# Nine instead of five column pairs of the up-projection by seven block products, their weight sums made earlier and parked in DRAM

## The chip, the cores and the metric

The kernel runs on one core of a Trainium2 chip. A core has a matmul engine (TensorE, PE in the profile), a vector engine (VectorE, DVE), a scalar engine (ScalarE, ACT), GpSimd (POOL), and a sync engine (SyncE, SP) whose queue issues most of the transfers between DRAM and the core's on-chip memory. Each engine works through its own queue; semaphores tie the queues together. [...]

The metric is the device time of one launch in microseconds: 726.13 us is the median of three runs before (726.13 to 726.62).

## What is computed

One block of a streaming encoder, for 512 frames of width 1024, all in float32:

```python
hn = rms_norm(x, norm1_g)
proj = hn @ w_in                  # q, k, v of branch A and of branch B, gates A and B
out_a = chunked_attention(qa, ka, va, ...)        # 8 heads x 64, softmax
out_b = stick_breaking_attention(qb, kb, vb)      # 8 heads x 64, strictly causal
mixed = sigmoid(gate_a) * (out_a @ w_branch_a) + sigmoid(gate_b) * (out_b @ w_branch_b)
x = x + mixed @ w_out
x = x + conv_glu(rms_norm(x, norm2_g), w_ffn_up, ffn_conv_w, ffn_conv_b, w_ffn_down)

def conv_glu(x, w_up, conv_w, conv_b, w_down):
    hid = x @ w_up                # 1024 -> 2 x 2816
    hid = causal_depthwise_conv(hid, conv_w) + conv_b      # width 3
    gate, up = hid[..., :D_FF], hid[..., D_FF:]
    return (silu(gate) * up) @ w_down
```

The change is in the line `hid = x @ w_up` and in the preparation of its weights.

## The kernel before

**Three matmuls for one.** Each float32 operand is split into a high half (a cast to the matmul's float32r format) and a low half (the rest), and each product is high by high, high by low, and low by high: three matmuls (`mm3`, L251). So each weight chunk of 128 x 2048 is loaded (`load`, L113, an SP transfer into one of two `raw` buffers) and then split: ScalarE copies it to `whi` and VectorE subtracts to get `wlo` (`split_gen`, L204). `run_chunk` (L242) runs the matmuls of one chunk and lets the split of the next chunk go on beside them; at the end of a split, `split_gen` issues the load of the chunk two ahead.

**Order of the chunks** (`_chunks`, L37): input projection and attention first, then `yB0`, `yB1` (the branch products), `wo0` to `wo3` (output projection), then `up0` to `up21`, and the 22 passes of the down-projection.

**Attention.** The loop at L726 goes through 64 steps, 32 for branch A and then 32 for branch B: eight heads by four blocks of 128 queries. A step has score matmuls, a chain on ScalarE and VectorE (softmax for A; two sigmoids, a reversed scan, a product and a mask on POOL for B, L622), transposes of the block on TensorE (L651), and the high and low halves of the transposed block (L664, L665). Steps start three ahead of their use. The chunks of the input projection are dealt out among the steps (`fill_gen`), so that TensorE has matmuls beside the chains. What belongs to a step is ranked 100 places ahead (`HP`).

**Up-projection.** Chunk `up{j}` holds 128 gate columns and the 128 up columns that go with them (a column pair). An ordinary pair (`up_body`, L935) is 2 x 8 x 3 = 48 matmuls with 512 frames as the moving operand. After it come the conv (`conv`, L849: one ScalarE pass, two VectorE passes each for gate and up), the SiLU, the product (L928), and for each two pairs the sums that the down-projection wants (`pair_sums`, L870). Seven of the eleven y sums are stored to DRAM by POOL (`ayd`, L933) and fetched back from j = 18 on (`fetch`, L948).

A pair in `SEVEN` (L63: 5, 8, 11, 14, 17) is done by seven block products in place of eight (`up_seven`, L986): the weights are taken as 2 x 2 blocks of 128 x 512 (two halves of the 1024 inputs by gate and up) and the frames as two halves of 256. Each product is 4 x 3 = 12 matmuls with 256 moving columns, so 84 in all, and five VectorE adds of 256 columns and four ScalarE copies put the results together. It needs three sums of weight blocks (S1, S2, S4) and one difference that takes the place of a block, and sums of the frames (`token_sums`, L960, made once during `up1` to `up3`). The weight sums are made by VectorE during the pair before (`block_sums`, L173, called at the end of the split of the pair before, L237), into the tile `sx`; `split_seven` (L188) then makes high and low halves of the four blocks (into `whi`, `wlo`) and of the three sums (into `wxh`, `wxl`). These are four VectorE sums of 512 columns, two more casts on ScalarE (1024 and 512 columns) and two more subtractions on VectorE than an ordinary pair has.

**Queues.** The order on each engine is laid down ahead of the run from the program's order, the ranks and the data dependences; at run time each engine follows its queue, and an instruction that waits holds those behind it. SP's queue has the weight loads, bias tiles, rows of x and results; POOL's the masks and the y sums.

Of the kernel before, what the change touches and what calls it, by code (L numbers as in the profile page):

```python
# [8 lines left out]
F32 = mybir.dt.float32  # L9
# [53 lines left out]
SEVEN = (5, 8, 11, 14, 17)  # L63
# [3 lines left out]
def block_kernel(ctx: ExitStack, tc: tile.TileContext, x, xt, params, g2, rbx, wts, wd0, wd1, out):  # L67
# [17 lines left out]
    pool_c = apool("pc")  # L85
    par = sm.tile([P, 280], F32, tag="par", name="par")
# [22 lines left out]
    raws, splits, late = {}, {}, {"halves": (), "casts": (), "products": ()}  # L109
# [3 lines left out]
    def load(i, parts=1):  # L113
# [14 lines left out]

        cuts = [0, *parts, 8] if isinstance(parts, tuple) else [8 * j // parts for j in range(parts + 1)]
# [43 lines left out]
    def block_sums(i):  # L173

        b = raws[i].rearrange("p (b c) -> p b c", c=512)
        sx = late["pool"].tile([P, 1536], F32, tag="sx", name=f"sx_{order[i]}")
        late["sx"] = sx
        s1, s2, s4 = (sx[:, 512 * j:512 * (j + 1)] for j in range(3))
        V.tensor_tensor(s1, b[:, 1], b[:, 3], op=ALU.add)
        yield  # L180
        V.tensor_tensor(s2, s1, b[:, 0], op=ALU.subtract)
        yield
        V.tensor_tensor(s4, b[:, 2], s2, op=ALU.subtract)
        yield
        V.tensor_tensor(b[:, 1], b[:, 0], b[:, 1], op=ALU.subtract)
        yield

    def split_seven(i, raw, hi, lo):  # L188

        key = order[i]  # L190
        wh, wl = (late["pool"].tile([P, 1600], F32R, tag=tag, name=f"{tag}_{key}")[:, 16:1552]
                  for tag in ("wxh", "wxl"))
        splits[key] = tuple(t.rearrange("p (k c) -> p k c", c=P) for t in (hi, lo, wh, wl))
        sx = late["sx"]
        for j, (h, l, src) in enumerate(((hi[:, 0:1024], lo[:, 0:1024], raw[:, 0:1024]),
                                         (wh[:, 0:1024], wl[:, 0:1024], sx[:, 0:1024]),
                                         (hi[:, 1024:2048], lo[:, 1024:2048], raw[:, 1024:2048]),
                                         (wh[:, 1024:1536], wl[:, 1024:1536], sx[:, 1024:1536]))):
            A.copy(h, src)
            V.tensor_tensor(l, src, h.bitcast(F32), op=ALU.subtract)  # L200
            if j < 3:
                yield

    def split_gen(i, pieces):  # L204
# [5 lines left out]
        raw = raws.pop(i)  # L210
        sh = 48 if key[:2] in ("qA", "kA", "vA", "vB") else 16 if key in ("up0", "up1") or is_seven(i) else 0
# [28 lines left out]
    pos = {k: i for i, k in enumerate(order)}  # L240
# [24 lines left out]
    ayd = dram.tile([7, P, 1536], F32, tag="ayd", name="ayd")  # L265

# [355 lines left out]
    def soft_b(h, t, ps):  # L622
# [8 lines left out]
        A.activation(b[:, :n], ps[:, :n], AF.Sigmoid, scale=rstd[:, t:t + 1])  # L631
# [74 lines left out]
    pend = []  # L706

# [18 lines left out]
    for s in range(len(steps)):  # L726
# [40 lines left out]
    for i in range(2):  # L767
        for _ in run_chunk(f"yB{i}", yB_body(i)):
            pass
# [56 lines left out]
    for c in range(3):  # L826
        for _ in run_chunk(f"wo{c}", wo_body(c)):
            pass
# [6 lines left out]
    for _ in sp:  # L835
        pass
    ap_ctx.close()
# [110 lines left out]
    def fetch(i):  # L948

        tag = {0: "sx", 1: "wxl"}.get(i, "ts" if i < 5 else "ax")  # L950
        n, bufs = {"sx": (1536, 1), "wxl": (1600, 1), "ts": (2048, 4), "ax": (2048, 8)}[tag]
# [299 lines left out]
```

## Time and profile before

| | |
|---|---|
| time, median of 3 runs | 726.13 us (726.13 to 726.62) |
| span of the profiled execution, first to last instruction | 724.9 us |
| TensorE busy / VectorE / ScalarE / POOL | 718.6 / 565.4 / 401.5 / 53.6 us |
| moved by DMA | 100.91 MB, mean 139 GB/s |
| TensorE's granted clock | 1.000 |

The time of the profiled execution as a whole is not among the records, only its span; the runs' median is 1.2 us above that span. Lines such as L254 are those of the listing above. A group's row gives the engine, the operation, output<-inputs by the names of their tiles, the shapes, the count, then the busy microseconds and the mean of one in nanoseconds, then the engine's idle time just before and what ended it. Rows of one tile give least, median and most nanoseconds instead. SPq is the queue on which SP issues transfers.

### The profile page before, as it was taken

What the parts mean: (1) busy time and instruction counts of PE and PEld (TensorE: products, weight loads), DVE (VectorE), ACT (ScalarE), POOL (GpSimd) and SP (SyncE); (2) the same over time, 40 slices, a digit from 0 to 9 for tenths busy, and PEclk for the clock granted to TensorE, in tenths of its full rate; (3) what the DMA queues carried; (4) which work ended last, traced back from release to release, by engine and by line L of the source; (5) the groups of instructions that cost most, each with busy time, mean ns of one, the idle gap of its engine ahead of it and who ended that gap; (6) DMA issues with size and microseconds to landing.
All of it is one profiled execution on the core that took longest, in us unless ns stands there. A gap on an engine that the chain in (4) does not pass through costs nothing.

```text
span 724.9 us, 10589 instructions
## 1 busy us (share of the span) xinstructions
PE 718.6 (99%) x4019; PEld 627.5 (87%) x4019; DVE 565.4 (78%) x1030; ACT 401.5 (55%) x727; POOL 53.6 (7%) x95
## 2 busy tenths in 40 slices
PE   8999999999999999999999999999999999999997
PEld 8999998888988888888889889889898988888886
DVE  6678867775988888566275799998979985997686
ACT  6675656657767676442254556655545653543541
POOL 2701200000101011000012000000000100000000
PEclk9999999999999999999999999999999999999999
DMA  8632232211313111314536613544335553564563
GB/s 308 250 131 78 83 117 74 74 59 58 118 63 113 59 59 59 136 68 144 195 149 239 203 62 156 186 135 160 118 145 186 181 184 117 173 243 174 177 222 116
DMA packets 24786, 100.91 MB, mean 139 GB/s; under 512 B 2592, under 2 KB 7328, under 8 KB 17184
## 3 DMA queue, kind: packets, MB, share of 16 engines
q1 hardware_dynamic: 21792, 87.00, 33.8%
q0 software_dynamic: 2656, 13.11, 5.0%
q8 instruction: 31, 0.51, 0.3%
q14 instruction: 19, 0.16, 0.1%
q10 hardware_dynamic: 288, 0.14, 0.1%
HBM read 88.44 MB, written 11.80 MB: 138 GB/s over the span
## 4 chain that ended last, share of the span: by engine, by line
PE 98%; DMA 1%; SPq 0%; DVE 0%; ACT 0%; DVEq 0%; issue 0%
PE P L1087 14%; PE p L998 7%; PE pg L254 4%; PE pg L253 4%; PE pg L255 4%; PE pu L254 4%; PE pu L255 4%; PE pu L253 4%; PE qkB L255 2%; PE gB L255 2%; PE qkB L253 2%; PE gA L253 2%; PE gA L254 2%; PE gB L253 2%; PE gA L255 2%; PE qkB L254 2%
## 5 line engine op out<-in xcount | busy, mean ns | idle before, releaser
L253 PE MATMUL pg<-hth,whi_up 128*128 128x512 f32 (+1 forms) x152 | 55.7, 367 | 0.0
L255 PE MATMUL pg<-hth,wlo_up 128*128 128x512 f32 (+1 forms) x152 | 55.7, 366 | 0.0
L254 PE MATMUL pg<-htl,whi_up 128*128 128x512 f32 (+1 forms) x152 | 55.7, 366 | 0.0
L254 PE MATMUL pu<-htl,whi_up 128*128 128x512 f32 (+1 forms) x152 | 55.6, 366 | 0.0
L253 PE MATMUL pu<-hth,whi_up 128*128 128x512 f32 (+1 forms) x152 | 55.6, 366 | 0.0
L255 PE MATMUL pu<-hth,wlo_up 128*128 128x512 f32 (+1 forms) x152 | 55.6, 365 | 0.0
L1087 PE MATMUL P<-whi_dn,ax 128*128 128x512 f32 x176 | 54.4, 389 | 0.0
L149 ACT CAST whi_dn<-raw_dn 128x1024 fp32r<-128x1024 f32 x33 | 34.3, 1051 | 25.5 <-PE P L1087 15.2
L145 DVE TENSOR_TENSOR wlo_dn<-raw_dn,whi_dn 128x1024 fp32r<-128x1024 f32 x33 | 40.0, 1224 | 9.2 <-ACT whi_dn L149 9.1
L228 DVE TENSOR_TENSOR wlo_up<-raw_up,whi_up 128x1024 fp32r<-128x1024 f32 (+1 forms) x40 | 41.2, 1062 | 7.0 <-ACT whi_up L226 7.0
L226 ACT CAST whi_up<-raw_up 128x1024 fp32r<-128x1024 f32 (+1 forms) x40 | 34.5, 917 | 14.7 <-PE pu L254 7.9
L1087 PE MATMUL P<-whi_dn,ay 128*128 128x512 f32 x132 | 40.8, 389 | 0.0
L1087 PEld LDWEIGHTS P<-whi_dn,ax 128*128 128x128 f32 x176 | 33.0, 188 | 6.8
L1087 PE MATMUL P<-wlo_dn,ax 128*128 128x512 f32 x88 | 34.2, 389 | 0.0
L254 PEld LDWEIGHTS pu<-htl,whi_up 128*128 128x128 f32 x152 | 28.6, 188 | 4.7
L253 PEld LDWEIGHTS pu<-hth,whi_up 128*128 128x128 f32 x152 | 28.5, 188 | 4.7
L255 PEld LDWEIGHTS pg<-hth,wlo_up 128*128 128x128 f32 x152 | 28.6, 188 | 4.7
L255 PEld LDWEIGHTS pu<-hth,wlo_up 128*128 128x128 f32 x152 | 28.5, 188 | 4.6
L253 PEld LDWEIGHTS pg<-hth,whi_up 128*128 128x128 f32 x152 | 28.6, 188 | 4.6
L254 PEld LDWEIGHTS pg<-htl,whi_up 128*128 128x128 f32 x152 | 28.6, 188 | 4.5
L633 DVE TENSOR_TENSOR_SCAN aB<-aB,reset 128x127 f32<-128x127 f32 (+3 forms) x32 | 26.0, 817 | 6.7 <-ACT aB L628 6.7
L1087 PEld LDWEIGHTS P<-whi_dn,ay 128*128 128x128 f32 x132 | 24.8, 188 | 5.1
(303 smaller groups left out, 2240.3 us busy)
## 6 DMA issues: line engine op xcount, KB each, us to landing
raw_up<-in_wts SPq DMA_DIRECT2D x22, 1024.0 KB, 4.8
raw_dn<-in_wd SPq DMA_DIRECT2D x11, 1024.0 KB, 4.8
raw_dn<-in_wd SPq DMA_DIRECT2D x11, 512.0 KB, 3.4
ayd<-ay POOLq DMA_DIRECT2D x7, 768.0 KB, 5.2
ay<-ayd POOLq DMA_DIRECT2D x7, 768.0 KB, 6.5
raw_gA<-in_wts SPq DMA_DIRECT2D x4, 1024.0 KB, 4.7
raw_qkB<-in_wts SPq DMA_DIRECT2D x4, 1024.0 KB, 4.8
raw_gB<-in_wts SPq DMA_DIRECT2D x4, 1024.0 KB, 4.7
```

What stands on the lines that cost most here:

```text
L145: chain("halves", V.tensor_tensor(o, x, y, op=op))
L149: chain("casts", A.copy(hi[:, sl], src))
L226: A.copy(hi[:, sl], raw[:, sl])
L228: E.tensor_tensor(lo[:, sl], raw[:, sl], hi[:, sl].bitcast(F32), op=ALU.subtract)
L253: PE.matmul(ps, sh, mh, start=first, stop=False)
L254: PE.matmul(ps, sh, ml, start=False, stop=False)
L255: PE.matmul(ps, sl, mh, start=False, stop=last)
L633: V.tensor_tensor_scan(ar, ar, reset[:, S - n:S - 1][:, ::-1], 1.0, op0=ALU.mult, op1=ALU.max)
L998: PE.matmul(ps, st, mv[:, k, :], start=first and k == 0 and n == 0, stop=last and k == 3 and n == 2, skip_group_check=True)
L1087: chain("products", PE.matmul(dst, st, mv, start=first and n == 0, stop=last and n == 2, skip_group_check=True))
```

## The change

1. `SEVEN` grows from (5, 8, 11, 14, 17) to (5, 7, 8, 10, 11, 12, 13, 15, 17): nine pairs are done by seven products, thirteen stay ordinary.
2. `block_sums` is gone. A new generator, `park_gen`, makes the sums of all nine pairs earlier, through one raw tile and one sum tile (`pkr`, `pks`). For a pair it loads the raw weights (1 MB), makes S1, the difference, S2 and S4 on VectorE, then three times a high half on ScalarE and a low half on VectorE, and stores the difference, the high halves and the low halves to a DRAM array `parked`.
3. One call of `park` makes one step of that generator (one load, one sum, or one cast with its subtraction), ranked 100 places behind. There is one call in each attention step from 8 to 49, two for each piece of `yB1` and of `wo0`, and one for each piece of `wo1` and `wo2`.
4. In the up-projection the raw load of a seven-product pair is three pieces (two blocks from the weights, the difference from `parked`), and `fetch_extra` loads the high and low halves of the sums (768 KB each) straight from `parked` into the tiles that TensorE reads. `split_seven` keeps only the halves of the four blocks.
5. The halves of pairs 7, 10 and 12 go into a second pair of tiles (`w2`), the others into `wxh` and `wxl`. For 5, 7, 8, 10 and 11 the fetch is issued at the end of the split of the pair before; for 12, 13, 15 and 17 (`LATE`) at the start of the pair's own split, which runs during the pair before. The first fetched y sum has a tile of its own (`wf`) in place of `sx`.

```diff
-SEVEN = (5, 8, 11, 14, 17)
+SEVEN = (5, 7, 8, 10, 11, 12, 13, 15, 17)
+EXTRA_AT = (7, 10, 12)
+LATE = (12, 13, 15, 17)
...
+        if is_seven(i):
+            n = SEVEN.index(i - pos["up0"])
+            SP.dma_start(raw[:, 0:512], wts[i, :, 0:512])
+            SP.dma_start(raw[:, 512:1024], parked[n, :, 0:512])
+            SP.dma_start(raw[:, 1024:2048], wts[i, :, 1024:2048])
+            yield
+            return
...
-    def block_sums(i):
-
-        b = raws[i].rearrange("p (b c) -> p b c", c=512)
-        sx = late["pool"].tile([P, 1536], F32, tag="sx", name=f"sx_{order[i]}")
...
+    def park_gen():
+
+        for n, j in enumerate(SEVEN):
+            i = pos[f"up{j}"]
+            raw = pool_pk.tile([P, 2048], F32, tag="pkr", name=f"pkr{j}")
+            sx = pool_pk.tile([P, 1536], F32, tag="pks", name=f"pks{j}")
+            behind(SP.dma_start(raw, wts[i]), (a_exps + b_sigs)[-1:])
+            yield
+            b = raw.rearrange("p (b c) -> p b c", c=512)
+            s1, s2, s4 = (sx[:, 512 * k:512 * (k + 1)] for k in range(3))
+            for o, x, y, op in ((s1, b[:, 1], b[:, 3], ALU.add), (b[:, 1], b[:, 0], b[:, 1], ALU.subtract),
+                                (s2, s1, b[:, 0], ALU.subtract), (s4, b[:, 2], s2, ALU.subtract)):
+                V.tensor_tensor(o, x, y, op=op)
+                yield
+            SP.dma_start(parked[n, :, 0:512], b[:, 1])
+            for k, (src, hi) in enumerate(((s1, b[:, 3]), (s2, b[:, 0]), (s4, b[:, 2]))):
+                A.copy(hi.bitcast(F32R), src)
+                V.tensor_tensor(src.bitcast(F32R), src, hi, op=ALU.subtract)
+                SP.dma_start(parked[n, :, 512 * (k + 1):512 * (k + 2)], hi)
+                yield
+            SP.dma_start(parked[n, :, 2048:3584], sx)
+
+    def fetch_extra(j):
+
+        n = SEVEN.index(j)
+        if j in EXTRA_AT:
+            wh, wl = (t[:, 16:1552] for t in late["w2"])
+        else:
+            wh, wl = (late["pool"].tile([P, 1600], F32R, tag=tag, name=f"{tag}_up{j}")[:, 16:1552]
+                      for tag in ("wxh", "wxl"))
+        SP.dma_start(wh.bitcast(F32), parked[n, :, 512:2048])
+        SP.dma_start(wl.bitcast(F32), parked[n, :, 2048:3584])
+        extras[j] = wh, wl
...
     def split_seven(i, raw, hi, lo):
...
+        wh, wl = extras.pop(i - pos["up0"])
+        splits[order[i]] = tuple(t.rearrange("p (k c) -> p k c", c=P) for t in (hi, lo, wh, wl))
+        for j in range(2):
+            sl = slice(1024 * j, 1024 * (j + 1))
+            A.copy(hi[:, sl], raw[:, sl])
+            V.tensor_tensor(lo[:, sl], raw[:, sl], hi[:, sl].bitcast(F32), op=ALU.subtract)
+            if j == 0:
                 yield
...
         raw = raws.pop(i)
+        if i - pos["up0"] in LATE:
+            fetch_extra(i - pos["up0"])
...
+        j = i + 1 - pos["up0"]
+        if j in SEVEN and j not in LATE:
+            fetch_extra(j)
         yield
-        if is_seven(i + 1):
-            yield from block_sums(i + 1)
...
+    def park():
+        with tc.high_priority(-LOW):
+            next(pk, None)
+
+    LOW = 100
...
+        if 8 <= s < 50:
+            park()
         br, h, t, e = pend.pop(0)
...
         for _ in run_chunk(f"yB{i}", yB_body(i)):
-            pass
+            if i == 1:
+                park()
+                park()
...
     for c in range(3):
         for _ in run_chunk(f"wo{c}", wo_body(c)):
-            pass
+            park()
+            if c == 0:
+                park()
...
+        late["w2"] = [fp.tile([P, 2048], F32R, tag="ax", name=f"w2{k}", bufs=8) for k in range(2)]
```

More of the change, by code (lines that the diff above doesn't have):

```diff
@@ L85, in block_kernel @@
     pool_c = apool("pc")
+    pool_pk = apool("ppk")
     par = sm.tile([P, 280], F32, tag="par", name="par")
@@ L107, in block_kernel @@
     order = [key for key, _, _ in CHUNKS]
-    raws, splits, late = {}, {}, {"halves": (), "casts": (), "products": ()}
+    pos = {k: i for i, k in enumerate(order)}
+    raws, splits, extras, late = {}, {}, {}, {"halves": (), "casts": (), "products": ()}
     FIRST_DN = order.index("dn0_0")
@@ L171, in is_seven @@
         return i < len(order) and order[i] in [f"up{j}" for j in SEVEN]
-    def block_sums(i):
-        b = raws[i].rearrange("p (b c) -> p b c", c=512)
-        sx = late["pool"].tile([P, 1536], F32, tag="sx", name=f"sx_{order[i]}")
[L177 to L186, printed above, removed]
@@ L188, in split_seven @@
-    def split_seven(i, raw, hi, lo):
[L190 to L201, printed above, removed]
+    def park_gen():
[18 more added lines that the diff above has]
+            SP.dma_start(parked[n, :, 2048:3584], sx)
@@ L265, in block_kernel @@
     ayd = dram.tile([7, P, 1536], F32, tag="ayd", name="ayd")
+    parked = dram.tile([len(SEVEN), P, 3584], F32, tag="parked", name="parked")
     reset = pool_c.tile([P, S], F32, tag="reset", name="reset")
@@ L836, in block_kernel @@
         pass
+    assert next(pk, 1) == 1
     ap_ctx.close()
```

8 lines of the change are left out of this document (4 added, 4 removed).

## The prediction

> **What bounds the kernel now.** I read the page first, then the waits of the matmul engine, then the chain of waits over the up-projection, and last the stages in which the added work falls. The page's first parts:
>
> ```profile
> span 724.9 us, 10589 instructions
> ...
> PE 718.6 (99%) x4019; PEld 627.5 (87%) x4019; DVE 565.4 (78%) x1030; ACT 401.5 (55%) x727; POOL 53.6 (7%) x95
> ```
>
> TensorE is busy for 99% of the span. A busy matmul engine could still be waiting between starts, so the second view is everything that it waited for, over the whole span:
>
> ```profile
> PE warm L301 <- DVE warm L298: 1.1, 1, 1.1
> PE qA L379 <- ACT whi_qA L226: 0.6, 1, 0.6
> PE qA L379 <- DVE whi_qA L224: 0.4, 1, 0.4
> ```
>
> All three lie in the first microseconds; after them TensorE waits for nobody. So the time is the sum of matmul starts: fewer or shorter matmuls are gained in full, and work elsewhere is free until it first makes TensorE wait. The chain of waits from 435 us to 565 us gives the two prices (start, length, what):
>
> ```profile
> 435.60 9.89 PE p L998 x84
> ...
> 467.28 9.89 PE p L998 x84
> ...
> 498.96 9.89 PE p L998 x84
> ```
>
> A seven-product pair is 84 matmuls in 9.89 us, 117.7 ns each. From one such pair to the next is 31.68 us both times (467.28 - 435.60, 498.96 - 467.28), with two ordinary pairs between: (31.68 - 9.89)/2 = 10.895 us for an ordinary pair of 48 matmuls, 227.0 ns each.
>
> **The change part by part.**
>
> *The matmuls (removed).* Columns 7, 10, 12 and 13 go from 48 wide to 84 narrow matmuls: 4 x (10.895 - 9.89) = 4.02 us less. All of it is on the path. 84 narrow ones at exactly half of 227.0 ns would be 9.53 us; the 0.36 us of dearer starts is already in the 9.89.
>
> [...]
>
> *Vector and scalar work taken out of the up-projection.* The durations (the last row, from the rows of one tile, has least, median and most in ns):
>
> ```profile
> L145 DVE TENSOR_TENSOR raw_dn<-raw_dn 128x512 f32<-128x512 f32 x22 | 15.2, 689 | 0.9 <-DMA raw_dn<-in_wd 0.6
> ...
> L226 ACT CAST whi_wo<-raw_wo 128x512 fp32r<-128x512 f32 x16 | 8.7, 618 | 17.0 <-PE wo L255 15.7 <-PE yB L254 1.3
> ...
> L200 DVE TENSOR_TENSOR wxl_up<-sx_up,wxh_up 128x1024 fp32r<-128x1024 f32 x5 | 6.1, 1224 | 0.0
> ...
> L199 ACT CAST wxh_up<-sx_up 128x1024 fp32r<-128x1024 f32 x5 | 5.2, 1040 | 1.8 <-DVE sx_up L181 1.8
> ```
>
> ```profile
> L1023 DVE TENSOR_TENSOR hu<-p,hu x5: 416/421/430, 448.4 to 573.9; 128x256 f32<-128x256 f32 x5
> ```
>
> Five pairs lose four sums (4 x 0.69) and two subtractions (1.22 + 0.69) on VectorE: 5 x 4.67 = 23.3 us; ScalarE loses 5 x (1.04 + 0.62) = 8.3 us. The four new pairs add five adds of 256 columns each on VectorE (4 x 5 x 0.42 = 8.4 us) and four copies of 256 on ScalarE (4 x 4 x 0.62 = 9.9 us at most, priced as if 512 wide). VectorE ends up with 15 us less in this stage, ScalarE with about as much. It is worth nothing, since TensorE waited for neither even here, where VectorE had no idle time at all (columns: window; window, PE, PEld, DVE, ACT, POOL busy; clock, DMA share, GB/s), at a clock of 1.00:
>
> ```profile
> 414.00:432.00 18.00, 18.00 (x81) 14.93 (x80) 18.00 (x24) 11.34 (x15) 0.00 (x0) 1.00 0.24 92
> 432.00:450.00 18.00, 18.00 (x121) 16.58 (x120) 18.00 (x32) 11.45 (x19) 0.54 (x1) 1.00 0.43 161
> 450.00:468.00 18.00, 18.00 (x85) 15.04 (x84) 18.00 (x29) 10.16 (x14) 0.53 (x1) 1.00 0.45 162
> 576.00:594.00 18.00, 18.00 (x81) 14.93 (x80) 16.37 (x25) 8.51 (x14) 0.54 (x1) 1.00 0.74 277
> ```
>
> These rows are also the cover for the four adjacent pairs 10 to 13: a full VectorE for 54 us cost TensorE nothing.
>
> *The same work added to attention and output projection.* Nine pairs, each with four sums and three subtractions of 512 columns on VectorE (7 x 0.69 = 4.8 us) and three copies on ScalarE (3 x 0.62 = 1.9 us): 43 us and 17 us in all. One park call makes about one VectorE instruction; 42 calls fall in attention steps 8 to 49, eight in yB1, 28 around wo0 to wo2. Where that lands (same columns), where the steps lie, and what one instruction costs when it follows another at once:
>
> ```profile
> 72.00:180.00 108.00, 108.00 (x641) 95.41 (x640) 77.83 (x215) 66.65 (x152) 4.77 (x8) 1.00 0.23 79
> 180.00:252.00 72.00, 72.00 (x412) 62.91 (x411) 62.44 (x114) 49.08 (x107) 8.22 (x19) 1.00 0.25 89
> 252.00:306.00 54.00, 54.00 (x272) 45.42 (x271) 40.54 (x71) 34.26 (x73) 4.58 (x11) 1.00 0.21 70
> ```
>
> ```profile
> L651 PE MATMUL pT_B<-ident,bB x80: 270/272/297, 181.1 to 297.5; 128*128 128x128 f32 x80
> ```
>
> ```profile
> 398.30 2.50 DVE L228 TENSOR_TENSOR wlo_up<-raw_up,whi_up 128x512 fp32r<-128x512 f32 x4 [0.67 <-ACT whi_up L226]
> ```
>
> The 32 B steps run from 181 to 297 us, 3.6 us each, so steps 32 to 49 end near 247 us. Four instructions in 2.50 us, the last 0.69, means 0.60 us each back to back. Calls 25 to 42 hold 15 sums or subtractions and three loads. VectorE in 180 to 252 us goes to 62.44 + 15 x 0.60 = 71.4 of 72 us, or 72.8 by the full 0.69; before it, 77.83 + 21 x 0.69 = 92.3 of 108. What does not fit can slide: after 252 us 13.5 us are idle. TensorE has a lead to live on, shown here where I found it shortest (a masked B block ready on POOL, and its transposes):
>
> ```profile
> 192.54 0.54 POOL L635 TENSOR_SCALAR_AFFINE_SELECT bB<-bB 128x128 f32<-128x128 f32 x2 [8.36 <-DVE bB L634]
> ```
>
> ```profile
> 194.83 0.71 PE L651 MATMUL pT_B<-ident,bB 128*128 128x128 f32 x5
> ```
>
> The first of the two ends near 192.8 us and is used at 194.8: 2.0 us, three parked instructions. Bounds of this part: nothing to 11.2 us (the slower rival below). I take nothing, by the 414 to 468 us rows, which are the nearest with a full VectorE; a gain is excluded, since no wait is there to remove. If the cover goes, the transposes of the B blocks are late first.
>
> *The transfers.* Sizes and landings:
>
> ```profile
> raw_up<-in_wts SPq DMA_DIRECT2D x22, 1024.0 KB, 4.8
> ...
> raw_dn<-in_wd SPq DMA_DIRECT2D x11, 512.0 KB, 3.4
> ayd<-ay POOLq DMA_DIRECT2D x7, 768.0 KB, 5.2
> ```
>
> ```profile
> L132 SPq DMA_DIRECT2D raw_up<-in_wts x5: 327/328/328, 471.0 to 513.4; - x5
> ```
>
> ```profile
> DMA to landing us min/median/max: 3.5/5.3/9.0
> ```
>
> The last row is for the 768 KB transfers of the y sums. Parking is six issues a pair on SP (54 in all), fetching two (18), and nine raw loads become three pieces (18 more): 90 x 0.33 us, spread over 600 us of a queue that waits most of the time. Parking moves 9 x 2.75 MB, fetching 9 x 1.5 MB. In the densest body (up12: two 768 KB halves for 13, one 1 MB load) that is 2.6 MB in 9.89 us, 265 GB/s; 277 GB/s was moved from 576 to 594 us with TensorE at its usual pace. The halves for 12 and 13 are issued when the body before begins and are first needed after its 9.89 us and one product (9.89/7 = 1.41): 11.3 us, against 9.0 for the slowest 768 KB landing. Bounds: nothing to 5.0 us (rival below); taken at nothing, by that landing.
>
> **Sum.** The profiled span 724.9 - 4.02 = 720.9 us. The median of the runs, 726.13, stands 1.2 us above that span, and I keep this distance: 722.1 us.
>
> **The rivals.**
>
> *VectorE cannot be packed in attention.* For it: no 18 us window of attention is above 16.40 of 18 us, 91%:
>
> ```profile
> 180.00:198.00 18.00, 18.00 (x136) 17.07 (x135) 16.40 (x31) 14.33 (x31) 2.75 (x5) 1.00 0.33 118
> ```
>
> At 91% the 72 us hold 65.6 us of work; 71.4 is wanted, 5.8 too much, less the lead of 2.0: 3.8 us, 725.9 if nothing slides past 252 us and less where it does. Against it: parked work is ranked 100 places back and has idle time later. Chance 0.13.
>
> *A parked sum at VectorE's head waits for its load (slower).* There is one raw and one sum buffer. The load waits on SP for the last halves to reach DRAM (3.4 us by the 512 KB row, a load of twice their size), lands 4.8 us later, and the first sum is written one step, 3.6 us, behind it: a wait of 1.2 us, up to 4.6. VectorE runs in order, so the scans, masks and lows of the next steps stand behind it, and the transposes behind those; SP's next weight load and bias tile stand behind the parked load. Three first sums fall in 180 to 252 us. The room is 72 + 2.0 - 71.4 = 2.6 us; waits of 2.9 us each (half way) take 8.7, so TensorE loses 6.1: 728.2 us. All 4.6 long they lose 11.2. It decides from 6.6 us of waits in this stretch, where the gain is gone. For it: such waits occur and are of this size (VectorE, whole span):
>
> ```profile
> DVE xT L971 <- DMA xT<-htd: 3.5, 1, 3.5
> ...
> DVE sx_up L179 <- DMA raw_up<-in_wts: 2.9, 1, 2.9
> ```
>
> Against it: these two cost TensorE nothing, and a sum ranked low may be placed well after its load. [...] Chance 0.11.
>
> *Late halves.* If the halves land behind a 1 MB load, 9.0 + 4.8 = 13.8 us against 11.3: 2.5 us each for 12 and 13, 5.0 in all, 727.1. Against it: the halves are issued ahead of that load. Chance 0.04.
>
> *Adjacent pairs are not 9.89 us.* Seven-product pairs stood alone so far. They take four of eight banks each, two bodies apart. If each of the four that follow at once (8, 11, 12, 13) waits for two late evacuations (2 x 0.42), 3.4 us go back: 725.5. Against it: two bodies are 19 us. Chance 0.06.
>
> **How the numbers follow.** The forecast has 0.66. The runs before lie within 0.5 us of each other, so its own range is 721.6 to 723.0. A measurement here tells about 0.2%, 1.45 us, from no change: 724.7 and 727.6. The packing rival is split about evenly between less and more than 2.6 us lost, the adjacent one lies mostly inside 1.45 us: faster 0.66 + 0.07 + 0.02 = 0.75; same 0.06 + 0.04 + 0.04 (late halves, 727.1) = 0.14; slower 0.11. The range 721.6 to 726.6 takes in the packing and adjacent rivals and leaves out the other two, 0.15, and a little below.
>
> **What would show it.** Right: nine runs of 84 matmuls at 9.89 us in the chain, 31.68 us shrinking to 20.8 us from 5 to 7 (9.89 + 10.9); no new row among TensorE's waits; VectorE near 70 of 72 us in the B half and under 18 in 414 to 468. Wrong: waits of TensorE for the blocks of the B branch or for the fetched halves, VectorE waiting for the parked raw tile, or a run of 84 longer than 9.89 us. What would make the prediction wrong is above all an order of VectorE's queue that puts parked sums ahead of their loads.

## The result, and the profile after

The changed kernel takes 732.01 us (median of 4 runs, 731.20 to 736.24) against 726.33 us before (726.13 to 726.62, 4 runs): ratio 1.009, 95% interval 1.0063 to 1.0116. It is slower by 5.7 us where 4 us less were forecast, and outside the range.

The head of the page after, and what TensorE waited for over the whole span (us in total, times, longest):

```profile
span 730.8 us, 11191 instructions
...
PE 718.7 (98%) x4163; PEld 633.1 (87%) x4163; DVE 591.0 (81%) x1083; ACT 412.2 (56%) x760; POOL 52.3 (7%) x95
```

```profile
PE yB L279 <- ACT oh_B L713: 2.3, 1, 2.3
PE p L1040 <- ACT pc L1045: 1.2, 1, 1.2
PE warm L328 <- DVE warm L325: 1.1, 1, 1.1
PE qA L406 <- ACT whi_qA L253: 1.0, 1, 1.0
PE pv_B L701 <- ACT pth_B L691: 0.6, 1, 0.6
PE s_A L622 <- DVE st L630: 0.5, 1, 0.5
...
```

The span grew by 5.9 us while TensorE's busy time hardly moved, and waits far from the start came in. (Line numbers after are some 25 to 45 higher than before; each experiment has its own.) To place them I took, for each slice of 18 us, the sum over all matmuls of the time to the next one's start, less the usual distance for its width (227 ns for 512 columns, 117.7 for 256; for the few narrower or between, the median of before). What is left I call lost:

```
us lost by TensorE, slice from     0     126   306+324   432+450   all others
before                             3.35  0.08   -0.06      0.06       -
after                              3.89  1.68    5.91      2.11       -
difference                        +0.5  +1.6    +6.0      +2.0      -0.2
```

Together +9.9, less the 4.02 saved, is the +5.9 of the span.

**The saving is there.** The chain of waits after (start, length, what) has the seven-product pairs at the forecast price, adjacent ones too (300 matmuls in 35.34 us, 117.8 ns each):

```profile
497.20 35.34 PE p L1040 x300
...
547.71 9.89 PE p L1040 x84
```

**The end of attention.** Windows of the changed kernel (window; window, PE, PEld, DVE, ACT, POOL busy; clock, DMA share, GB/s):

```profile
72.00:180.00 108.00, 107.00 (x633) 93.99 (x632) 88.28 (x231) 66.74 (x152) 3.85 (x6) 1.00 0.43 157
180.00:252.00 72.00, 72.00 (x401) 62.78 (x400) 62.54 (x114) 48.44 (x103) 5.48 (x15) 1.00 0.43 154
198.00:216.00 18.00, 18.00 (x97) 15.43 (x96) 17.97 (x35) 11.30 (x26) 1.39 (x4) 1.00 0.42 161
252.00:306.00 54.00, 54.00 (x274) 45.70 (x273) 46.05 (x83) 37.27 (x80) 5.52 (x14) 1.00 0.49 174
270.00:288.00 18.00, 18.00 (x91) 15.22 (x90) 17.94 (x32) 15.07 (x31) 1.58 (x2) 1.00 0.48 162
322.00:324.30 2.30, 0.06 (x1) 0.00 (x0) 1.58 (x4) 1.19 (x2) 0.00 (x0) 0.95 0.72 180
324.30:327.40 3.10, 3.09 (x7) 2.51 (x8) 1.23 (x2) 0.00 (x0) 0.00 (x0) 0.50 0.98 317
```

From 180 to 306 us TensorE is busy throughout and waits for nobody. VectorE is full in two of the seven stretches of 18 us, from 198 and from 270 us, and between 13.7 and 16.5 us busy in the other five. Its parked instructions do not stand one to a step: in attention they are six groups of seven, one pair each, that begin at 88.0, 134.8, 170.4, 199.9, 237.6 and 272.2 us and last 7 to 12 us. The fourth and the sixth group fall into the two full stretches. Beside the second group TensorE waits twice for VectorE, 0.54 us at 136.85 and 0.46 us at 138.18. And the last masked block of B leaves POOL (timeline, start and length first) 24 us later than before, first before and then after:

```profile
292.62 0.29 POOL L635 TENSOR_SCALAR_AFFINE_SELECT bB<-bB 128x128 f32<-128x128 f32 x1 [7.30 <-DVE bB L634]
```

```profile
316.73 0.29 POOL L662 TENSOR_SCALAR_AFFINE_SELECT bB<-bB 128x128 f32<-128x128 f32 x1 [7.28 <-DVE bB L661]
```

What filled TensorE meanwhile is the other work that before was left for the end, the gB columns. Before, the last gB matmul starts 7.5 us after the last of B's (TensorE's timeline):

```profile
304.19 0.27 PE L674 MATMUL pv_B<-ptl_B,v_vB 128*128 128x128 f32 x1
...
311.64 0.39 PE L255 MATMUL gB<-hth,wlo_gB 128*128 128x512 f32 x1
```

Now the last gB matmul starts at 309.74 us, the yB groups that can run are used up by 318.4, and the last B matmul starts at 321.74. Then nothing is left (the same, after):

```profile
309.74 0.39 PE L281 MATMUL gB<-hth,wlo_gB 128*128 128x512 f32 x1
...
321.74 0.33 PE L701 MATMUL pv_B<-ptl_B,v_vB 128*128 128x128 f32 x1 [0.25 <-DVE ptl_B L692]
324.31 1.65 PE L279 MATMUL yB<-oh_B,whi_yB 128*128 128x512 f32 x3 [2.25 <-ACT oh_B L713]
325.76 0.63 PE L280 MATMUL yB<-ol_B,whi_yB 128*128 128x512 f32 x1
...
327.71 0.39 PE L281 MATMUL yB<-oh_B,wlo_yB 128*128 128x512 f32 x1
```

The wait of 2.25 us has a sequel: for the next 3.1 us the granted clock is 0.50 and matmuls that start every 227 ns elsewhere start every 425 to 430. Three shorter waits (0.61, 0.26 and 0.25 us) stand in the 5 us before it. Which of the four the lower clock needs, and what ends it, no run shows.

**At 449 us.** ScalarE's timeline: the cast of the next y waits 3.66 us until the y store before it, in the same buffer, is done, and the copies that TensorE needs stand behind it. The store itself (in the chain, 10.19 us) was 3.5 us before:

```profile
448.72 0.40 ACT L949 CAST ax<-st 128x256 fp32r<-128x256 f32 x1
452.79 0.40 ACT L949 CAST ay<-ub 128x256 fp32r<-128x256 f32 x1 [3.66 <-DMA ayd<-ay]
...
453.83 0.36 ACT L1045 COPY pc<-p 128x256 f32<-128x256 f32 x1
```

```profile
442.57 10.19 DMA ayd<-ay
```

It runs beside the raw pieces of pair 7 (issued from 440.0 us) and its two fetched halves (from 441.3): in its 10.19 us the DMA share is 0.91, at 322 GB/s.

### The profile page after: what moved, and what is told of

The parts are those of the page before. It is cut to its first block, busy times and chain, and to the rows that moved or that the text cites. A ratio compares the mean times of both kernels' runs of the same rounds, so it can differ in the third digit from the quotient of the medians.

```text
span 730.8 us, 11191 instructions
## 1 busy us (share of the span) xinstructions
PE 718.7 (98%) x4163; PEld 633.1 (87%) x4163; DVE 591.0 (81%) x1083; ACT 412.2 (56%) x760; POOL 52.3 (7%) x95
## 4 chain that ended last, share of the span: by engine, by line
PE 88%; DVE 4%; DMA 3%; ACT 2%; SPq 1%; issue 1%; DVEq 0%; ACTq 0%
PE P L1129 14%; PE p L1040 11%; PE pu L279 2%; PE pg L281 2%; PE pu L281 2%; PE pu L280 2%; PE pg L279 2%; PE pg L280 2%; PE gB L281 2%; PE gA L279 2%; PE gA L280 2%; PE gB L280 2%; PE gB L279 2%; PE wo L280 2%; PE wo L281 2%; PE wo L279 2%
## 5 line engine op out<-in xcount | busy, mean ns | idle before, releaser
L279 PE MATMUL pg<-hth,whi_up 128*128 128x512 f32 (+1 forms) x120 | 43.3, 362 | 0.4 <-DVE cg L895 0.4
L281 PE MATMUL pg<-hth,wlo_up 128*128 128x512 f32 (+1 forms) x120 | 43.3, 360 | 0.0
L280 PE MATMUL pu<-htl,whi_up 128*128 128x512 f32 (+1 forms) x120 | 43.2, 360 | 0.0
L280 PE MATMUL pg<-htl,whi_up 128*128 128x512 f32 (+1 forms) x120 | 43.2, 360 | 0.0
L279 PE MATMUL pu<-hth,whi_up 128*128 128x512 f32 (+1 forms) x120 | 43.2, 360 | 0.0
L281 PE MATMUL pu<-hth,wlo_up 128*128 128x512 f32 (+1 forms) x120 | 43.1, 359 | 0.0
L691 ACT CAST pth_A<-pT_A 128x128 fp32r<-128x128 f32 (+2 forms) x40 | 14.7, 372 | 22.5 <-PE pT_A L678 14.8
L1040 PE MATMUL p<-ts,whi_up 128*128 128x256 f32 x144 | 26.3, 281 | 0.0
L279 PE MATMUL qkB<-hth,whi_qkB 128*128 128x512 f32 x64 | 25.5, 398 | 0.5 <-DVE v_vB L438 0.5
L1129 PE MATMUL P<-wlo_dn,ay 128*128 128x512 f32 x66 | 25.8, 391 | 0.0
L279 PEld LDWEIGHTS pg<-hth,whi_up 128*128 128x128 f32 x120 | 22.6, 188 | 3.7 <-ACT ax L949 0.6
```

What stands on the lines that cost most here:

```text
L279: PE.matmul(ps, sh, mh, start=first, stop=False)
L280: PE.matmul(ps, sh, ml, start=False, stop=False)
L281: PE.matmul(ps, sl, mh, start=False, stop=last)
L691: A.copy(view(ph), src)
L1040: PE.matmul(ps, st, mv[:, k, :], start=first and k == 0 and n == 0, stop=last and k == 3 and n == 2, skip_group_check=True)
L1129: chain("products", PE.matmul(dst, st, mv, start=first and n == 0, stop=last and n == 2, skip_group_check=True))
```

## The experiments

In the expectations, A is the theory that the parked work in attention makes the loss (A1: by VectorE's time; A3: by VectorE waiting for the parked loads; A5: by the sums that stand in the last steps; A6: VectorE has room for part of it), A4 is that work moved to POOL holds up the masks there. B is the theory that the slow y store makes the loss at 449 us, S and S2 that the buffers added in DRAM and on chip slow the start. "Lost" is by the measure of the table above. The label in brackets (e0, e1 and so on) is the name by which later parts call a run.

### Parts of the parked work alone

**One pair parked** (e0), its data fetched for all nine (the sums and halves of the other eight are left out):

```diff
-        for n, j in enumerate(SEVEN):
+        for n, j in enumerate(SEVEN[:1]):
```

> Only the first of the nine pairs is parked, and all nine pairs fetch its halves and its difference, so the weight sums of the other eight are left out; the up-projection has the same instructions and transfers as the changed kernel. Theory A (the parked work in attention is what was lost between 126 and 342 us, some 7.5 us, and the rest, 2 us, near 449 us, belongs to the up-projection): 724 to 725 us, the stalls at 136, 318 to 327 us gone, that at 449 to 454 us still there. Rival (the denser up-projection itself pushes work back into the stages before, or nine pairs are not worth 4 us): 727 us or more.

724.72 us (724.11 to 726.78), ratio 0.9986 [0.9976, 0.9995]. No wait in attention, nothing lost at 306 to 342 us, and the time is within A's 724 to 725. A holds.

**All transfers and casts, no VectorE work** (e1; the four sums and three subtractions of each pair are left out):

```diff
-                V.tensor_tensor(o, x, y, op=op)
...
-                V.tensor_tensor(src.bitcast(F32R), src, hi, op=ALU.subtract)
```

> Every parked step keeps its load, its casts on ScalarE and its stores, but the sums and subtractions on VectorE are left out (the parked halves are raw blocks). Theory A1 (VectorE's load delays the attention chain until its tail stands bare): the losses at 136 and 318 to 327 us go, 724 to 725 us. Rival A2 (the transfers, SP's queue or ScalarE's casts delay the chain): they stay, 730 to 732 us.

724.91 us (723.64 to 727.25), ratio 0.9988 [0.9978, 0.9997], with the DMA engines as loaded in attention as in the changed kernel (159 and 179 GB/s against 157 and 154) and 0.2 us lost from 306 to 342:

```profile
72.00:180.00 108.00, 108.00 (x644) 95.52 (x643) 77.69 (x215) 70.21 (x160) 4.74 (x8) 1.00 0.45 159
180.00:252.00 72.00, 72.00 (x410) 62.95 (x409) 63.17 (x116) 52.14 (x114) 7.54 (x19) 1.00 0.47 179
```

So transfers, issues on SP and casts in attention cost next to nothing, as predicted; VectorE's 63 instructions are what costs. But they are not without effect: the last transposes of B start at 304.1 us in place of 297.5, and the work left for the end shrinks (the table of the next section).

**All VectorE work, no transfers** but the first pair's (e2; the transfers of the other eight are left out, and all nine use one raw and one sum tile):

```diff
-            behind(SP.dma_start(raw, wts[i]), (a_exps + b_sigs)[-1:])
+            if n == 0:
+                behind(SP.dma_start(raw, wts[i]), (a_exps + b_sigs)[-1:])
```

> The reverse: all sums, subtractions and casts stay, on one tile, but only the first pair is loaded and stored (all nine fetch it); the other parked transfers are left out, and with them every wait of VectorE for a parked load. Theory A1: the tail at the end of attention is still bare, 729 to 732 us. Rival A3 (the prediction's slower rival: sums that wait at VectorE's head for their load): 724 to 726 us.

748.84 us (747.51 to 751.61), ratio 1.0317 [1.0295, 1.0340], far over what any theory expected. Without loads to wait for, all 63 instructions stand between 88 and 178 us, where only 21 stood in the changed kernel; VectorE is at 92% and TensorE waits in earnest, 12.8 us of 108, the clock down to 0.95 with it:

```profile
72.00:180.00 108.00, 95.18 (x545) 82.61 (x544) 99.49 (x241) 64.02 (x141) 3.84 (x6) 0.95 0.30 101
```

```profile
PE pT_A L683 <- DVE eA L642: 5.7, 2, 5.0
PE pT_A L683 <- DVE ptl_A L697: 3.6, 1, 3.6
PE s_B L627 <- ACT bB L663: 3.5, 1, 3.5
...
```

A3 falls: the loads did not hold VectorE up, they spread its work out. In the changed kernel VectorE waits for a parked load only once, 0.7 us, and that behind attention. What A1 expected, a bare end, did not come either: 0.15 us are lost there, and the loss is where the instructions are crowded.

### The same work elsewhere

**The last attention pair moved behind attention** (e7; calls at steps 8 to 47 in place of 8 to 49):

```diff
-        if 8 <= s < 50:
+        if 8 <= s < 48:
```

> Parking stops after attention step 47 instead of 49, so that five whole pairs are parked in attention and the sixth, whose sums stood among the last steps of attention, moves behind it; nothing is left out and the fetches are those of the changed kernel. Theory A5 (the sums of the sixth pair stand in the tail itself and hold its last casts): the loss of 318 to 327 us falls from 5.9 to 1 us or less, 726.5 to 728 us. Theory A1 (all 36 instructions make the chain late little by little, and TensorE's other work runs out): about a seventh less, 730.5 to 731.5 us.

732.11 us (731.40 to 733.68), ratio 1.0091 [1.0074, 1.0108]; 5.75 us lost at 306 to 342 us as before. A5 falls: the sums seen beside the bare end are not its cause; it is made earlier.

**The four sums on GpSimd** (e5), and then **sums and subtractions on GpSimd** (e6; both with the fetch for pair 7 called one body earlier, as in e4 of the next part):

```diff
-                V.tensor_tensor(o, x, y, op=op)
+                G.tensor_tensor(o, x, y, op=op)
```

> As the run with the early fetch, and the four sums of each parked pair are made on POOL (1.30 us for 512 columns by the wlo_vA row of before), so VectorE keeps three of seven instructions a pair, about 15 of the 36 in attention. Theory A1 (VectorE's load alone): most of the 7.5 us lost in attention goes, 723.5 to 725.5 us. Rival A4 (the load only moves the bound: parked sums stand ahead of the masks of the B steps in POOL's queue): 728 us or more.

> As before, with the three subtractions on POOL too: VectorE has no parked work, POOL seven instructions a pair. Theory A1: as without VectorE's parked work and without the stall near 449 us, 723 to 724.5 us. Rival A4: slower than the run with the sums alone on POOL, since 36 instead of 21 parked instructions stand among the masks.

729.45 us (ratio 1.0045 [1.0028, 1.0063]) and 731.22 us (1.0072 [1.0047, 1.0097]). The bare end is gone (0.28 and 0.24 us lost there), but 4.6 and 4.9 us go between 72 and 306 us, against 1.0 before. Both times are as A4 had them, but only one wait of TensorE there, 1.4 us in e5, is for a mask; those in e6 (1.6 us in two, and 0.9) are for VectorE. VectorE, with no parked instruction, is busier than before between 72 and 180 us: 88.42 us against 77.83. Its groups in that window (busy us, mean ns of one), before and with all on GpSimd:

```profile
L228 DVE TENSOR_TENSOR wlo_gA<-raw_gA,whi_gA 128x512 fp32r<-128x512 f32 x16 | 10.4, 685 | 0.0
...
L665 DVE TENSOR_TENSOR ptl_A<-pT_A,pth_A 128x384 fp32r<-128x384 f32 x12 | 6.6, 550 | 0.0
```

```profile
L255 DVE TENSOR_TENSOR wlo_gA<-raw_gA,whi_gA 128x512 fp32r<-128x512 f32 x16 | 16.4, 1060 | 0.0
L694 DVE TENSOR_TENSOR ptl_A<-pT_A,pth_A 128x384 fp32r<-128x384 f32 x13 | 7.1, 546 | 0.0
```

`wlo_gA`, with both inputs in the on-chip memory (SBUF), goes from 685 to 1060 ns on average: six of the sixteen, all beside a parked instruction on GpSimd, take 1.30 to 1.78 us, the others 0.67 to 0.70. `ptl_A`, with one input in the memory of the matmul results (PSUM), has 546 after 550. In e1, with the same transfers and casts and no GpSimd sums, the first has 683 ns. By what the two engines get in each other's way no run shows.

### The loss at 449 us

**Fetches a body later** (e3; LATE extended to pairs 7, 8, 10 and 11), and **the fetch for 7 called a body earlier** (e4):

```diff
-LATE = (12, 13, 15, 17)
+LATE = (7, 8, 10, 11, 12, 13, 15, 17)
```

```diff
+        if j == 6:
+            fetch_extra(7)
```

> The fetches of pairs 7, 8, 10 and 11 are issued one body later, in the body just before their use, as for 12 to 17. Theory B (near 449 us the store of the first y sum takes 10.2 us beside the fetch for pair 7, ScalarE waits 3.7 us for its single tile and holds the copies that free the products): the store takes 4 to 7 us, the 2 us near 449 us go, 729.5 to 730.5 us. Rival B2 (VectorE's backlog after the token sums holds TensorE there): nothing changes there, 732 us.

> The two halves for pair 7 are fetched one body earlier, during up4 instead of up5, where little is transferred; nothing else changes. Theory B (the first y store is slow beside that fetch and ScalarE waits for its tile): the store takes 4 to 7 us instead of 10.2, the 2 us near 449 us go, 729.5 to 730.5 us. Rival B2 (a backlog of VectorE holds TensorE there): 731.5 to 732.5 us.

733.93 us (1.0099 [1.0080, 1.0118]) and 733.33 us (1.0100 [1.0085, 1.0115]). Issued later, the halves leave the y store alone (4.76 us), as B had it, and the loss near 449 us is mostly gone (0.76 us from 432 to 450), but TensorE then waits 1.7 us for late halves further on. The second edit did not do what it was meant to: the halves stand behind pair 7's raw pieces in SP's queue and still went out at 443.1 us, beside the y store (9.52 us). It tells nothing of B.

**Two buffers for y** (h1; the later fetch of the first y takes the second one):

```diff
-            ay = fp.tile([P, 1536], F32R, tag="ay", name=f"ay{i}")
+            ay = fp.tile([P, 1536], F32R, tag="ay", name=f"ay{i}", bufs=2)
```

> The changed kernel with two buffers for the y halves of a pair (the fetch of the first of them later uses the second buffer, in place of its own tile), nothing else. Theory B (the y store near 442 us, slowed to 10 us, holds ScalarE at the cast of the next y, and TensorE waits for its copies): ScalarE does not wait for a y store, no loss at 449 to 454 us, 1.5 to 2.1 us under the changed kernel, 729.5 to 730.5. Rival (ScalarE is late there for another reason): the loss at 450 us stays and the time is that of the changed kernel within 0.5 us.

732.07 us (730.63 to 733.91), ratio 1.0077 [1.0063, 1.0091]. ScalarE no longer waits for the y store, though that still takes 9.4 us, and the loss from 432 to 468 us falls from 2.11 to 1.07. The median did not move; the profiled execution, the slowest of the five (733.91 us), lost 5.98 us at the start (next part). So B holds for half of the 2 us; the other half, a wait for VectorE's cg, stays without it. With a store as slow, e0 and e1 lose 0.7 and 0.9 us there (9.26 and 9.71 us) and e6 2.5 (10.04), so the store alone does not set the size of this loss; what else does stays open.

### The start

Every kernel with the change loses 3.9 to 6.1 us in the first 18 us, against 3.35 before, because the second piece of raw_qA lands at 7.9 to 8.8 us in place of 7.13. Two additions to the kernel before: **the DRAM scratch**, one piece of it written once (f0), and **the on-chip buffer**, used by nothing (g0).

```diff
+    parked = dram.tile([9, P, 3584], F32, tag="parked", name="parked")
...
+    pool_pk = apool("ppk")
+    pkr = pool_pk.tile([P, 3584], F32, tag="pkr", name="pkr")
```

> The kernel before with a DRAM tile of the size of the parked one (9 x 128 x 3584 floats), of which one piece of 256 KB is written in the output projection and never read; nothing else differs. Theory S (the scratch that the changed kernel adds in DRAM makes the first loads land later): the second piece of raw_qA lands near 8 us in place of 7.1, TensorE loses some 4.1 to 4.6 us in its first 18 us in place of 3.35, and the time is 0.7 to 1.2 us over that of before (ratio near 1.0013). Rival (the start is slower for another reason of the changed program): 3.35 us lost at the start and the time of before within 0.3 us.

> The kernel before with the on-chip buffer of the parked work (14 KB a partition) set aside in the same place and used by nothing; no instruction differs. Theory S2 (the moved addresses of the buffers make the first loads land later): the second piece of raw_qA lands near 8.4 us in place of 7.1 to 7.2, TensorE loses some 4.2 us in its first 18 us in place of 3.0 to 3.35, the time rises by about 1 us. Rival (something else of the changed program): start and time as before within 0.4 us.

726.22 us (ratio 1.0000 [0.9991, 1.0009]) and 726.04 us (0.9998 [0.9990, 1.0007]); the piece lands at 7.24 and 7.03 us. Neither alone is the cause. It stays open.

### How much attention takes, and where

Some of the nine pairs were made in place again, as before the change, and fewer parked. **Four parked, all behind attention** (f1); the same **with pair 7's halves ahead of its raw pieces** (f2); **five parked, all behind attention** (g1); and **five parked, 16 of the calls in attention** (g2), at every second step from 8 to 38:

```diff
+PARK = (7, 10, 12, 15)
-        if 8 <= s < 50:
-            park()
```

```diff
+        if i == pos["up0"] + 4:
+            fetch_extra(7)
```

```diff
+PARK = (7, 10, 12, 13, 15)
-        if 8 <= s < 50:
+        if 8 <= s < 40 and s % 2 == 0:
```

> All nine pairs of the change stay, but five of them (5, 8, 11, 13, 17) make their sums and halves in the up-projection as before, and only four (7, 10, 12, 15) are parked, all behind attention, in the last stage of branch B and the output projection. Theory A (parked work in attention is the loss; the nine pairs are worth 4.0 us): attention as in before, no wait of TensorE at 136 and at 318 us, 4.0 us saved in the up-projection, about 1 us lost at the start and 1 to 2 us at 450 us: span 721.5 to 723, time 723 to 724.5, ratio 0.996 to 0.998. Rival (VectorE was full in the up-projection and the five pairs in place, closer together than before, make TensorE wait there): 725 to 728, with waits p <- halves between 480 and 560 us.

> The kernel with four parked pairs, with the halves of pair 7 fetched ahead of the raw pieces of pair 7 on SP, one body earlier, so that they do not share the DMA engines with the first y store. Theory B (the y store slowed by these halves holds back ScalarE at 450 us): the y store near 442 us takes 4 to 6 us in place of 10, the loss at 449 to 454 us falls by 1 to 2 us, and the time is 1 to 2 us under that of f1_mix. Rival (the y store is slow by itself or the wait of ScalarE there has another cause): the same loss at 450 us and the time of f1_mix within 0.5 us.

> All nine pairs; 5, 8, 11 and 17 make sums and halves in the up-projection as before, and 7, 10, 12, 13 and 15 are parked, all behind attention. Theory A (parked work in attention is the loss, the pairs themselves give 4.0 us): attention as in before, no wait at 136 and 318 us, at most 1 us lost between 450 and 560 us, about 1 us at the start and 1 us near 380 us: span 721.5 to 723.5, time 723.5 to 725, ratio 0.996 to 0.998. Rival (VectorE is too full in the up-projection, or the parked work behind attention costs there): 726 to 729, with waits of TensorE on the halves between 480 and 560 us or at 380 us.

> As g1_mix5, but 16 of the 41 parked calls (two pairs: 14 VectorE instructions with their loads, casts and stores) stand in attention, one at every second step from 8 to 38, and so many fewer behind it. Theory A1 (each step of attention has its chain through VectorE, and any added work makes it slip in proportion): VectorE busier by some 9 us between 72 and 250 us, a third of the loss of the changed kernel: 2 to 3 us over g1_mix5. Rival A6 (VectorE has slack in attention for part of the work, and only the full dose of one call a step overruns it): no wait of TensorE in attention and the time of g1_mix5 within 0.6 us.

730.34 us (1.0056 [1.0043, 1.0068]), 729.73 us (1.0051 [1.0039, 1.0063]), 736.92 us (1.0154 [1.0140, 1.0167]) and 729.00 us (1.0044 [1.0029, 1.0060]). All four have a clean attention, the last with 14 parked VectorE instructions in it. f1 and g1 did not come to A's 723 to 725 us. All four lose in the up-projection instead, 5.0, 4.9, 7.2 and 6.6 us from 500 to 540 us, where pair 11 in place stands between parked neighbours. That g2 is 7.9 us under g1, neither A1 (2 to 3 us over it) nor A6 (level with it) had. In g2, ScalarE waits 2.97 us at 520 us for a y store once more, TensorE 2.4 us for its cast, and the clock is at 0.50 for 5 us. With pair 7's halves well ahead (second kernel), or behind it (first), the y store at 442 to 444 us takes 4.07 and 3.83 us in place of 10.19: the neighbour transfers do slow it, and f2 had nothing to gain over f1.

**Nine parked, 24 calls in attention**, over all steps (h2) or over the first 32 (h3), two buffers for y, the rest of the calls doubled up behind attention:

```diff
-        if 8 <= s < 50:
+        if 8 <= s < 50 and s % 7 in (1, 3, 5, 6):
```

```diff
+        if 8 <= s < 40 and s % 4 != 3:
```

> As h1_two_ay, with 24 of the 42 parked calls in attention, four in every seven steps, and the other 18 moved behind it (two at each turn of the last stage of B and of the output projection). Theory A1 (any added work makes attention slip in proportion): 24/42 of the loss in attention stays, some 4 us, 725.5 to 727.5. Rival A6 (VectorE has slack for part of it): no wait of TensorE at 318 us, at most 1 us lost in attention, 722.5 to 724.5, under the kernel before.

> As h2_spread24, with the 24 calls at three of every four steps from 8 to 39 and none in the last ten steps. If the place decides (the slip of the first half has time to be made up before the end of attention): the waits near 136 us are those of the changed kernel, some 1.4 us, and none at 318 us, 723.5 to 725. If only the dose decides: the time of h2_spread24 within 0.6 us.

738.11 us (1.0164 [1.0150, 1.0178]) and 745.65 us (1.0263 [1.0249, 1.0277]), worse than any theory had it, most of it through the work that was moved behind attention. In attention h2 loses 4.6 us at the end, near the 4 us that A1 gave for 24 of 42 calls, so that A6 falls for this share; h3, with as many calls, loses 1.7 there, so the place counts beside the number. In the second a parked sum stands at VectorE's head until its load lands (VectorE's timeline), the lows of the up-projection's input behind it, and TensorE waits 4.1 us:

```profile
397.16 0.69 DVE L196 TENSOR_TENSOR pks<-pkr 128x512 f32<-128x512 f32 x1 [4.32 <-DMA pkr<-in_wts]
397.77 1.28 DVE L346 TENSOR_TENSOR htl<-tp_n,hth 128x512 fp32r<-128x512 f32 x2
```

In the first, the up-projection's buffers lie where the parked sums were, and ScalarE waits for the last of those to reach DRAM (its timeline):

```profile
423.40 0.78 ACT L891 ACTIVATE cg<-pg,par 128x512 f32<-128x512 f32 x1 [9.80 <-DMA parked<-pks]
```

**Eight pairs** (g5): five parked, 16 calls in attention, pair 11 as plain columns again.

```diff
-SEVEN = (5, 7, 8, 10, 11, 12, 13, 15, 17)
+SEVEN = (5, 7, 8, 10, 12, 13, 15, 17)
```

> As g2_mix5_half with eight pairs by seven products in place of nine: pair 11 is computed as two plain columns, so that 5, 8 and 17 are made in place and 7, 10, 12, 13 and 15 parked, 16 of the parked calls in attention. Theory A (a pair saves 1.0 us wherever VectorE and ScalarE keep pace): three pairs more than before save 3.0 us, no loss in attention, none near 523 us, some 1 us lost at the start: span 722 to 723.5, time 723.8 to 725.2, ratio 0.997 to 0.999. Rival (the y stores beside the halves hold back ScalarE also without pair 11, or the saving is eaten elsewhere): a wait of over 1 us in the up-projection and 726 us or more.

724.47 us (723.93 to 726.24), ratio 0.9980 [0.9969, 0.9990]: 1.9 us under before. Three pairs are 3.0 us; 0.8 go at the start, and no wait is left beyond it:

```profile
PE qA L440 <- ACT whi_qA L285: 2.2, 1, 2.2
PE warm L362 <- DVE warm L359: 1.1, 1, 1.1
```

## What the runs say of the end of attention

Each matmul has a place in the order in which TensorE ran them. For the last B transpose and the last gB matmul it is given here, counted over all matmuls of the trace from the first, with the number of parked VectorE instructions between 72 and 316 us and the time lost from 306 to 342 us:

```
                    last B transpose   last gB matmul   parked   lost, us
before                    1840              1905           0      -0.06
g5_eight                  1840              1905          14      -0.05
e1_no_vector              1866              1905           0       0.21
e2_no_park_dma            1883              1897          63       0.15
h3_early24                1886              1897          21       1.66
h2_spread24               1915              1893          21       4.62
e7_five_pairs             1924              1893          35       5.75
after                     1924              1878          42       5.91
```

Wherever the gB work stands ahead of B's last transposes, the end is bare (4.62 to 5.91 us lost); where 14 or more matmuls lie from them to the last gB, it is not (0.21 at most); 11 are not quite enough (1.66). That explains why TensorE showed no wait from 180 to 306 us while B slipped by 24 us: the last transposes of B stand 84 places later and start 21 us later. It is no simple function of the number of parked instructions: 14 between 88 and 175 us (g5) leave the order as it was, with 21 between 88 and 194 us (h3) 11 places are left, and with 21 between 89 and 225 us (h2) the last gB is ahead. e1 shows that without VectorE's work the end stays covered, though the transfers and casts alone use up 26 of the 65 places. A full VectorE is not needed for it: h2 has the bare end, and VectorE is at most 17.4 us busy in any stretch of 18 us there. Whether the old order of TensorE could have run with all 42 of them was not tried.

## Why the prediction was wrong, step by step

- **The matmuls, 4.02 us: right.** 9.89 us a pair, adjacent or alone; with eight pairs and clean neighbours the saving arrives, less the start. The rival of dearer adjacent pairs is refuted; its eight banks are the eight tiles for matmul results that the kernel takes (L276 to L279), four of them for a pair (L988).
- **VectorE's work in attention at nothing, "by the 414 to 468 us rows, which are the nearest with a full VectorE": this step failed.** It cost 7.6 us (1.6 at 136 us, 6.0 at the end). A full VectorE was free in the up-projection of before, where by the program it makes the weights' halves for the body that follows. In attention each step goes through VectorE on its way back to TensorE, and the place of its instructions counts, not its idle share over the stage: VectorE was at 87% from 180 to 252 us before and after (62.44 and 62.54 us), where I had it at 71.4 of 72; 14 parked instructions do stand there, and the kernel's own moved out. I had one parked instruction to a step and 36 in attention; there were 42, in groups of seven.
- **"What does not fit can slide": it slid, but with B's steps.** Those came 24 us later, and I had not asked what TensorE would still have to do by then. The lead of 2.0 us that I took for the shortest says nothing of it; the cover that counted were the 7.5 us of gB behind B's last matmul.
- **The packing rival** (chance 0.13, 725.9) named the right engine and stage but bounded it by VectorE's share, 3.8 us lost. Its limit of 91% does not hold: VectorE was busy for 17.97 of 18 us from 198 us on. The loss was twice that, and most of it came as a bare end, half clock included, some 30 us after the last such stretch.
- **The slower rival**, a parked sum waiting for its load in attention, did not happen there: VectorE waits for no parked load in attention, and without loads attention got worse (e2). It does exist where the calls stand closer: behind attention it cost 4 us in h3.
- **Transfers at nothing: failed at one place, 2.0 us.** I asked whether the halves land in time, and they did. I did not ask what they do to others: the y store between them took 10.2 us, and the single y buffer made ScalarE pay. Half of it is that (h1); the other half is a wait for VectorE whose cause stays open.
- **The distance from span to time**, kept at 1.2 us, is 1.7 us in the changed kernel (732.50 against 730.8) and in f0, which differs from before only by its scratch (726.09 against 724.4); later executions of before with the span of 724.9 took 726.6. The 0.5 us at the start were unforeseen, and their cause stays open.

## What to carry to other kernels

Work is not free because its engine has idle time (VectorE was at 62.44 of 72 us from 180 us on, and the parked work cost 7.6 us): ask for each stage whether the bound engine waits, within a step, for that engine's result, and how much unrelated work of the bound engine is left at the end of the stage, in its own order. When work moves to another stage, list what shares its queue, its buffers and its DMA engines there; the y store at 449 us and the two losses behind attention in h2 and h3 came from such neighbours. A kernel that moves part of the work (eight pairs, 14 of 42 instructions) can gain where the whole loses.

## What was not expected of the hardware

- GpSimd beside VectorE: in e6 a GpSimd sum of 128x512 took 1.35 to 1.54 us on average between 72 and 180 us, and VectorE's `wlo_gA`, of that size and with two SBUF inputs, rose from 685 to 1060 ns, so that VectorE was busier without the parked work than before (88.42 against 77.83 us).
- A wait of 2.25 us for TensorE, after a few short ones, cost 3.1 us at half clock behind it, some 1.5 us more; in g2, 2.4 us and then 0.9 cost 5 us at half clock.
- The first y store (768 KB) took 3.5 to 4.8 us where no fetch of halves was issued just ahead of it (before, e3, f1, f2, g2, g5), and 9.3 to 10.2 us behind two halves and the raw pieces of pair 7 (after, e0 to e2, e4 to e7, h1).
